# Weight rows stored as even and odd columns 2 KB apart, and read alternately by the products

## The chip, the cores and the metric

One core of one Trainium2 chip. The metric is the device time of one execution in microseconds (us); the kernel before was run three times. One further execution was taken by the hardware profiler: "the profile" and "the trace" mean that one.

## The reference

Two layers on a sequence of 256 frames with 2048 features; all inputs are float32. Each layer normalises, projects to 4096-wide parts, attends over 32 heads of 128, gates, projects back and adds to the residual. Cut to what matters:

```python
# first layer
h = rms_norm(x, a_norm)
q, k, v, g = jnp.split(h @ a_w_in, 4, axis=-1)             # 2048 -> 4 x 4096
o = chunked_relbias_attention(q, k, v, a_rel_bias)
x = x + (o * jax.nn.silu(g)) @ a_w_out                      # 4096 -> 2048
# second layer
h_kv = rms_norm(x, kv_norm)
k_s, v_s = jnp.split(h_kv @ kv_w, 2, axis=-1)               # 2048 -> 2 x 4096
cum_logf_h = cumsum(log_sigmoid(h_kv @ f_w + f_b))
q, g = jnp.split(rms_norm(x, b_norm) @ b_w_in, 2, axis=-1)  # 2048 -> 2 x 4096
o = forgetting_attention(q, k_s, v_s, cum_logf_h)
x = x + (o * jax.nn.silu(g)) @ b_w_out                      # 4096 -> 2048
return rms_norm(x, final_norm)
```

The projections are nearly all of the arithmetic. A product of float32 exactness is made of three products: each operand is split into a high part (rounded to the type fp32r) and a low part (the rest), and high x high, high x low and low x high are added up.

## The kernel before, in words

**The products.** The transposed activations are held on chip as high and low parts for the whole kernel (`Stat`: `xT`, `oA`, `x1T`, `oB`) and are the stationary operands, 128 x 128. The weights stream past them as the moving operand, 512 columns at a time (`UN`). `mm3` (lines 169 to 179) issues, for one row block of K (128 deep), the three products for each of the two halves of the sequence (`NT`): six matmuls at line 177. A `Unit` is 512 output columns with two accumulators; its `step` (346) takes one block of two rows of K (`KB`), and calls `mm3` for each.

**The weights' way.** The host cuts each weight matrix into units and blocks (`_units`, 958), so that one block is [128 partitions, 2 rows of K, 512 columns], 4 KB per partition in one run. `Feed` holds a list `todo` of all blocks in the order of use, written out at lines 306 to 334. `load` (190) issues a block's DMA from SyncE's queue into one of three `raw` tiles. `prepare` (211) splits it: ScalarE copies to the high part and VectorE subtracts (237, 238); in the second layer both also scale by the norm's gain, per row of K (233, 234). Four pairs of split tiles let TensorE run behind. A few blocks of the last projection are kept (`keep`).

**Quads.** In 15 of the 16 head groups of each layer the last block of both units is worked by a seven-product scheme (Strassen's, in a variant) in place of eight: `load_quad` (252) brings the two blocks side by side into `quad_raw`, `differ` (258) and `quad` (269) form differences and split them, and `products` (603) issues the 21 matmuls through `dot3` (426).

**Order.** The order of the work is fixed by the program: `drive` (682) and `project` (369) step the units, and between the steps advance the attention of the head group before (`attention`, 431), whose products are 256 or 128 columns wide. Nothing else sets it but the semaphores between the engines.

Of the kernel before, what the change touches and what calls it, by code (L numbers as in the profile page):

```python
# [9 lines left out]
F32 = mybir.dt.float32  # L10
F32R = mybir.dt.float32r
BF16 = mybir.dt.bfloat16
AF = mybir.ActivationFunctionType
OP = mybir.AluOpType
AX = mybir.AxisListType

P = 128
S = 256
NT = S // P
# [15 lines left out]
GC = HG * DH  # L35
UN = 512
KB = 2
SQ = 32
NQ = P // SQ
RAW = 3  # L40
SPLIT = 4
# [21 lines left out]

def r32(ap):
    return ap.bitcast(F32)


@with_exitstack
def trunk(ctx, tc, x, x_t, gains, a_w_in, a_rel, a_w_out, kv_w, f_w, f_b, b_w_in, b_w_out, final_norm, out):
# [5 lines left out]
    stream = ctx.enter_context(tc.tile_pool(name="stream", bufs=3))  # L75
# [9 lines left out]
    def big_tile(shape, dt, name):  # L85
        return big.tile(shape, dt, name=name, tag="big")
# [94 lines left out]
    class Feed:  # L181
# [8 lines left out]
        def load(self, spec, b, first):  # L190
            if self.early:
                raw = self.early.pop(0)
            else:
                raw = stream.tile([P, KB, UN], F32, name=f"{spec['name']}_raw{b}", tag="raw", bufs=RAW)
            for j in range(KB) if first else [slice(None)]:
                if first:
                    first(j)
                sp.dma_start(out=raw[:, j], in_=spec["w"][b][:, j])
            return raw

        def begin(self, first=None):
# [9 lines left out]
        def prepare(self, ahead=True, parts=(slice(None),)):  # L211
            if not self.loaded:
                self.begin()
            if not self.loaded:
                return
            spec, b, raw, (before, behind) = self.loaded.pop(0)
            if spec == "quad":
                self.quad(*b)
                self.refill()
                return  # L220
            if before:
                before()
            nm, h = spec["name"], b - (spec["nk"] // KB - spec["late"])
            if 0 <= h < spec["kept"]:
                both = big_tile([P, 2, KB, UN], F32R, f"{nm}_keep{b}")
                hi, lo = both[:, 0], both[:, 1]
            else:
                hi = stream.tile([P, KB, UN], F32R, name=f"{nm}_hi{b}", tag="hi", bufs=SPLIT)
                lo = stream.tile([P, KB, UN], F32R, name=f"{nm}_lo{b}", tag="lo", bufs=SPLIT)
            if spec["g0"] is not None:  # L230
                for j in range(KB):
                    gk = gain[:, spec["g0"] + b * KB + j:][:, :1]
                    act.activation(hi[:, j], raw[:, j], AF.Copy, scale=gk)  # L233
                    dve.scalar_tensor_tensor(lo[:, j], raw[:, j], gk, r32(hi[:, j]), op0=OP.mult, op1=OP.subtract)  # L234
                parts = ()
            for j in parts:
                act.activation(hi[:, j], raw[:, j], AF.Copy)  # L237
                dve.tensor_sub(lo[:, j], raw[:, j], r32(hi[:, j]))  # L238
            if behind:
                behind()  # L240
            self.ready.append((hi, lo))
            if ahead:
                self.refill()
# [8 lines left out]
        def load_quad(self, layer, g):  # L252
            q = quads[layer]
            for r in range(2):
                self.behind(q.raw[:, r, :, :1], -1)
                sp.dma_start(out=q.raw[:, r], in_=q.w(r, g))

        def differ(self, layer):

            q = quads[layer]  # L260
            raw, t = q.raw, q.t
            for r in range(2):
                for j in range(KB) if q.g0 else ():
                    act.activation(raw[:, r, j], raw[:, r, j], AF.Copy,
                                   scale=gain[:, q.g0[r] + QUAD * KB + j:][:, :1])
            dve.tensor_sub(t[:, 0], raw[:, 1], raw[:, :, 0])
            dve.tensor_sub(raw[:, 1, 0], raw[:, 1, 1], t[:, 0, 0])

        def quad(self, layer, i):


            raw, t = quads[layer].raw, quads[layer].t
            src = [raw[:, 0], t[:, 0], raw[:, 1, 1:], raw.rearrange("p a b n -> p (a b) n")[:, 1:3]][i]
            n = src.shape[1]
            hi = stream.tile([P, KB, UN], F32R, name=f"quad_hi{i}", tag="hi", bufs=SPLIT)
            lo = stream.tile([P, KB, UN], F32R, name=f"quad_lo{i}", tag="lo", bufs=SPLIT)
            act.activation(hi[:, :n], src, AF.Copy)
            dve.tensor_sub(lo[:, :n], src, r32(hi[:, :n]))
            if not i:
                dve.tensor_sub(raw[:, 0, 1], raw[:, 0, 1], raw[:, 1, 0])  # L280
            self.ready.append((hi, lo))

        def behind(self, dst, n):

            act.activation(dst, r32(self.ready[n][0][:, :, :1]), AF.Copy)

        def fill(self):
            while len(self.ready) <= DEPTH:
# [48 lines left out]
    class Unit:  # L337
# [8 lines left out]
        def step(self, b):  # L346
            hi, lo = feed.get()
            hold = b >= self.nk // KB - self.late
            if hold:
                self.held.append((b, hi, lo))  # L350
            for j in range(KB):
                mm3(self.acc, self.lhs, b * KB + j, range(1 if hold else NT), hi[:, j], lo[:, j], self.nk,
                    self.begun)
            self.left -= 1
            if not self.left:
                for b, hi, lo in self.held:
                    for j in range(KB):
                        mm3(self.acc, self.lhs, b * KB + j, [1], hi[:, j], lo[:, j], self.nk, self.begun)

    def unit(lhs):  # L360
        yield from rest(Unit(lhs, next(order)))
# [155 lines left out]
        return gs  # L517


    quad_raw, quad_t = (big_tile([P, 2, KB, UN], F32, name=f"quad{i}") for i in range(2))  # L520
    for both in (quad_raw, quad_t):
        feed.early += [both[:, 0], both[:, 1]]
    comb = big_tile([P, 2 * NT, UN], F32, name="comb")
    sums = big_tile([P, 2, 2, 4, P], F32R, name="sums")
    sq = [comb.rearrange("p a (k s) -> p (a k) s", s=S),
          quad_t.rearrange("p a b (k s) -> p (a b k) s", s=S)]
    xT = Stat("xT", KD)
    xr, homes = {}, iter(["wideh", "tb", "widel", "oT", "gs", "R", "Y", "Z", "wideh"])

# [48 lines left out]
    class Quads:  # L578
# [3 lines left out]
        def __init__(self, lhs, raw, t, comb, sums, w, g0=None):  # L582
            self.lhs, self.raw, self.t, self.comb, self.sums, self.w, self.g0 = lhs, raw, t, comb, sums, w, g0
            self.home = [v.rearrange("p (i c u) -> p i c u", i=NQ, u=SQ) for v in
                         (t[:, 1].rearrange("p b n -> p (b n)"), sums[:, 1].rearrange("p a k s -> p (a k s)"))]

        def sums_of_x(self):

# [14 lines left out]
        def products(self, first, second, scaled):  # L603


            comb = self.comb

            def x(k, t):
                return [v(QUAD * KB + k)[:, t * P:(t + 1) * P] for v in (self.lhs.h, self.lhs.l)]

            def sx(i):
                return self.sums[:, 0, 0, i], self.sums[:, 0, 1, i]

            def prod(acc, a, w, j, stop):
                dot3(acc, a, [v[:, j] for v in w], stop, stop)

            p1, p5, p7, p6 = (bank(n) for n in ("p1", "p5", "p7", "p6"))
            w = feed.get()
            prod(p1, x(0, 0), w, 0, True)
            prod(first.acc[0], x(1, 0), w, 1, False)  # L620
            w = feed.get()
            prod(p5, sx(0), w, 0, True)
            prod(p7, sx(2), w, 1, True)
            w = feed.get()
            dot3(second.acc[0], sx(3), [v[:, 0] for v in w], True, False)
            second.begun.add(0)
            w = feed.get()
            prod(first.acc[1], x(1, 1), w, 0, False)
            prod(p6, sx(1), w, 1, True)
            act.activation(comb[:, 0], p1, AF.Copy)  # L630
            dve.tensor_add(comb[:, 3], comb[:, 0], p6)
            dve.tensor_add(comb[:, 2], comb[:, 3], p5)
            dve.tensor_add(comb[:, 1], comb[:, 3], p7)
            dve.tensor_add(comb[:, 3], comb[:, 1], p5)
            rs, places = scaled
            for i, c1 in places:
                act.activation(comb[:, i, :c1], comb[:, i, :c1], AF.Copy, scale=rs[:, i % NT:i % NT + 1])
# [199 lines left out]
        yield  # L837


    b_tiles = [big_tile([P, 2, KB, UN], F32, name=f"b_quad{i}") for i in range(2)]  # L840
    b_tiles += [big_tile([P, 2 * NT, UN], F32, name="b_comb"), big_tile([P, 2, 2, 4, P], F32R, name="b_sums")]
    qb = quads["b"] = Quads(x1T, *b_tiles, lambda r, g: (b_w_in, kv_w)[r][g][QUAD], (GB, GKV))
    oB = Stat("oB", KI)
# [114 lines left out]
def _units(w, starts):  # L958

    k = w.shape[0] // P  # L960
    out = []
    for parts in starts:
        n = UN // len(parts)
        cols = np.concatenate([w[:, c:c + n] for c in parts], axis=1)
        out.append(cols.reshape(k // KB, KB, P, UN).transpose(0, 2, 1, 3))
    return np.ascontiguousarray(np.stack(out))


# [28 lines left out]
```

## Time and profile before

| | before |
|---|---|
| time, median of 3 runs | 1832.77 us (1830.29 to 1833.8) |
| span of the profiled execution | 1826.7 us |
| profiled execution's own time beside its span | not given by the page |
| mean granted TensorE clock | 0.998 |
| bytes moved, mean rate | 396.38 MB, 217 GB/s |

The engines are named as on the page: PE is TensorE's matmuls, PEld its weight loads, DVE is VectorE, ACT ScalarE, POOL GpSimd, SP SyncE. In a row of the groups stand the line, the engine, the operation, output and inputs, the shapes, the number of instructions, then the busy time in us, the mean length of one in ns, and the idle time of the engine just before them. A matmul's length there is from its start to its end, and successive matmuls overlap, so the distance between starts, not the length, is what one costs in a stream.

### The profile page before, as it was taken

To read this page: it belongs to the slowest core of one execution; us is meant where nothing else is said; L and a number is where in the kernel's file an instruction comes from. 1 tells how busy PE (TensorE), PEld (TensorE's weight loads), DVE (VectorE), ACT (ScalarE), POOL (GpSimd) and SP (SyncE) were. 2 spreads that over 40 slices of the span, in tenths; PEclk is the share of its full clock that TensorE was granted. 3 is DMA by queue.
4 is the path that set the end of the run, shared out by engine and by line. 5 is a ranking of instruction groups with operands and counts; after the bars stand their busy time and mean duration, and the time that the engine had idled before them with its cause. 6 is when DMAs were issued, how large, how long until landed. Compare 5 with 4: busy or idle time off the path is not lost.

```text
span 1826.7 us, 26015 instructions
## 1 busy us (share of the span) xinstructions
PE 1813.0 (99%) x8297; PEld 1507.2 (83%) x8297; DVE 1423.8 (78%) x2094; ACT 1196.3 (65%) x2245; POOL 521.8 (29%) x1071
## 2 busy tenths in 40 slices
PE   9999999999999999999999999999999999999998
PEld 7888888888888888888888888888888888888886
DVE  7887888888888787655568889888898989886544
ACT  6666666666666566545558777778777877775443
POOL 1333333333333333111104333333333333333000
PEclk9999999999999999999999999999999999999999
DMA  8666676666666766677766666666666666666664
GB/s 287 224 224 211 214 223 216 222 215 215 218 210 219 223 206 198 210 231 227 235 202 217 220 215 220 205 224 220 209 225 218 221 211 224 216 218 221 200 210 155
DMA packets 143145, 396.38 MB, mean 217 GB/s; under 512 B 31104, under 2 KB 37536, under 8 KB 142880
## 3 DMA queue, kind: packets, MB, share of 16 engines
q1 hardware_dynamic: 106960, 354.25, 59.0%
q0 software_dynamic: 32256, 37.29, 6.6%
q10 hardware_dynamic: 3792, 3.17, 0.6%
q8 instruction: 66, 1.08, 0.3%
q14 instruction: 71, 0.58, 0.1%
HBM read 351.05 MB, written 4.23 MB: 194 GB/s over the span
## 4 chain that ended last, share of the span: by engine, by line
PE 61%; DVE 1%; DMA 1%; ACT 1%; issue 1%; ACTq 0%; SPq 0%; DVEq 0%
PE bqg_acc L177 16%; PE bkv_acc L177 15%; PE bo_acc L177 10%; PE ao_acc L177 10%; PE avg_acc L177 2%; PE aqk_acc L177 2%; PE p L428 1%; PE p L429 1%; PE p L427 1%; DMA bqg_raw<-in_b_w_in 1%; PE op L485 1%; DVE bqg_lo L234 0%; PE s0p L451 0%; PE bqg_acc L429 0%; PE bqg_acc L428 0%
## 5 line engine op out<-in xcount | busy, mean ns | idle before, releaser
L400 POOL DMA_DIRECT2D sgZ<-sgY x512 | 250.5, 497 | 494.7 <-PE bkv_acc L177 188.1
L237 ACT ACTIVATE avg_hi<-avg_raw 128x1024 fp32r<-128x1024 f32 x112 | 118.5, 1058 | 125.8 <-DMA avg_raw<-in_a_w_in 82.8
L234 DVE SCALAR_TENSOR_TENSOR bkv_lo<-bkv_raw,gain,bkv_hi 128x512 fp32r<-128x512 f32 x226 | 159.2, 743 | 37.5 <-ACT bkv_hi L233 37.2
L238 DVE TENSOR_TENSOR avg_lo<-avg_raw,avg_hi 128x1024 fp32r<-128x1024 f32 x112 | 136.7, 1221 | 50.4 <-ACT avg_hi L237 49.9
L177 PE MATMUL bqg_acc<-bqg_hi,x1Th 128*128 128x512 f32 x452 | 174.1, 396 | 0.0
L177 PE MATMUL aqk_acc<-aqk_hi,xTh 128*128 128x512 f32 x452 | 172.4, 393 | 1.0 <-ACT aqk_hi L237 1.0
L233 ACT ACTIVATE bqg_hi<-bqg_raw,gain 128x512 fp32r<-128x512 f32 x226 | 150.3, 713 | 34.8 <-DMA bqg_raw<-in_b_w_in 18.0
L234 DVE SCALAR_TENSOR_TENSOR bqg_lo<-bqg_raw,gain,bqg_hi 128x512 fp32r<-128x512 f32 x226 | 162.7, 766 | 12.7 <-ACT bqg_hi L233 12.2
L177 PE MATMUL avg_acc<-avg_hi,xTh 128*128 128x512 f32 x452 | 172.3, 393 | 0.0
L177 PE MATMUL bqg_acc<-bqg_hi,x1Tl 128*128 128x512 f32 x452 | 171.4, 390 | 0.0
L177 PE MATMUL aqk_acc<-aqk_lo,xTh 128*128 128x512 f32 x452 | 170.9, 390 | 0.4 <-DVE aqk_lo L238 0.4
L177 PE MATMUL aqk_acc<-aqk_hi,xTl 128*128 128x512 f32 x452 | 171.0, 390 | 0.0
L177 PE MATMUL avg_acc<-avg_hi,xTl 128*128 128x512 f32 x452 | 170.9, 390 | 0.0
L177 PE MATMUL bkv_acc<-bkv_hi,x1Th 128*128 128x512 f32 x452 | 170.9, 390 | 0.0
L177 PE MATMUL bkv_acc<-bkv_hi,x1Tl 128*128 128x512 f32 x452 | 170.7, 389 | 0.0
L177 PE MATMUL bkv_acc<-bkv_lo,x1Th 128*128 128x512 f32 x452 | 170.6, 389 | 0.0
L177 PE MATMUL avg_acc<-avg_lo,xTh 128*128 128x512 f32 x452 | 170.6, 389 | 0.0
L177 PE MATMUL bqg_acc<-bqg_lo,x1Th 128*128 128x512 f32 x452 | 170.6, 389 | 0.0
L238 DVE TENSOR_TENSOR aqk_lo<-aqk_raw,aqk_hi 128x1024 fp32r<-128x1024 f32 x110 | 133.2, 1223 | 46.0 <-ACT aqk_hi L237 45.5
L233 ACT ACTIVATE bkv_hi<-bkv_raw,gain 128x512 fp32r<-128x512 f32 x226 | 150.1, 712 | 21.0 <-DMA bkv_raw<-in_kv_w 13.9
L400 POOL DMA_DIRECT2D b_sums<-b_quad x256 | 125.4, 498 | 132.3 <-PE bqg_acc L177 52.9
L400 POOL DMA_DIRECT2D sums<-quad x192 | 94.2, 498 | 206.4 <-PE avg_acc L177 79.8
(318 smaller groups left out, 4378.1 us busy)
## 6 DMA issues: line engine op xcount, KB each, us to landing
bqg_raw<-in_b_w_in SPq DMA_DIRECT2D x113, 512.0 KB, 4.0
bkv_raw<-in_kv_w SPq DMA_DIRECT2D x113, 512.0 KB, 4.7
avg_raw<-in_a_w_in SPq DMA_DIRECT2D x112, 512.0 KB, 5.2
aqk_raw<-in_a_w_in SPq DMA_DIRECT2D x110, 512.0 KB, 4.2
ao_raw<-in_a_w_out SPq DMA_DIRECT2D x64, 512.0 KB, 3.6
bo_raw<-in_b_w_out SPq DMA_DIRECT2D x64, 512.0 KB, 4.3
sgZ<-sgY POOLq DMA_DIRECT2D x512, 40.0 KB, 3.8
quad<-in_a_w_in SPq DMA_DIRECT2D x32, 512.0 KB, 5.9
```

What stands on the lines that cost most here:

```text
L177: pe.matmul(acc[t], x[:, t * P:(t + 1) * P], w, start=t not in begun, stop=k == nk - 1 and i == 2)
L233: act.activation(hi[:, j], raw[:, j], AF.Copy, scale=gk)
L234: dve.scalar_tensor_tensor(lo[:, j], raw[:, j], gk, r32(hi[:, j]), op0=OP.mult, op1=OP.subtract)
L237: act.activation(hi[:, j], raw[:, j], AF.Copy)
L238: dve.tensor_sub(lo[:, j], raw[:, j], r32(hi[:, j]))
L400: queues[j].dma_start(out=r32(z)[j * SQ:(j + 1) * SQ, i], in_=y[i * SQ:(i + 1) * SQ, j])
L427: pe.matmul(out_, a[0], b[0], start=start, stop=False)
L428: pe.matmul(out_, a[0], b[1], start=False, stop=False)
L429: pe.matmul(out_, a[1], b[0], start=False, stop=stop)
L485: pe.matmul(op[:, i, P:], v1[:, i * DH:(i + 1) * DH], pT[:, i, NT], start=False, stop=i == HG - 1)
```

## The change

Each row of 512 weights is stored as its 256 even columns and its 256 odd ones, and in a block of two rows of K the even halves of both rows stand first. A tile `[P, KB, UN]` becomes `[P, IL, KB, HN]` with `IL` = 2 and `HN` = 256: in a partition the run is even columns of row 0, even of row 1, odd of row 0, odd of row 1, 1 KB each. So columns 2n and 2n + 1 of a row lie 2 KB apart. The host stores the weights in that order (`_units`), so a block's transfer is the same 4 KB per partition. The new function `cols` hands a row to the matmul as the pattern (n, a): 256 times an even and an odd one in turn. The accumulators get their columns in the order of before, and nothing behind them changes. Splits of a whole block stay one run; where one row of K is split or scaled by itself, its two runs of 256 lie 2 KB apart. The quads' raw tile holds both blocks' even halves ahead of the odd ones (`[P, IL, 2, KB, HN]`), so that its rows too have their halves apart.

The core of the diff (the quads' differences and the first tiles are re-indexed in the same way and left out):

```diff
+IL = 2
+HN = UN // IL
...
+def cols(v, j):
+
+    return v[:, :, j].rearrange("p a n -> p n a")
...
-                raw = stream.tile([P, KB, UN], F32, name=f"{spec['name']}_raw{b}", tag="raw", bufs=RAW)
+                raw = stream.tile([P, IL, KB, HN], F32, name=f"{spec['name']}_raw{b}", tag="raw", bufs=RAW)
...
-                sp.dma_start(out=raw[:, j], in_=spec["w"][b][:, j])
+                sp.dma_start(out=raw[:, :, j], in_=spec["w"][b][:, :, j])
...
-                both = big_tile([P, 2, KB, UN], F32R, f"{nm}_keep{b}")
+                both = big_tile([P, 2, IL, KB, HN], F32R, f"{nm}_keep{b}")
...
-                hi = stream.tile([P, KB, UN], F32R, name=f"{nm}_hi{b}", tag="hi", bufs=SPLIT)
-                lo = stream.tile([P, KB, UN], F32R, name=f"{nm}_lo{b}", tag="lo", bufs=SPLIT)
+                hi = stream.tile([P, IL, KB, HN], F32R, name=f"{nm}_hi{b}", tag="hi", bufs=SPLIT)
+                lo = stream.tile([P, IL, KB, HN], F32R, name=f"{nm}_lo{b}", tag="lo", bufs=SPLIT)
...
-                    act.activation(hi[:, j], raw[:, j], AF.Copy, scale=gk)
-                    dve.scalar_tensor_tensor(lo[:, j], raw[:, j], gk, r32(hi[:, j]), op0=OP.mult, op1=OP.subtract)
+                    act.activation(hi[:, :, j], raw[:, :, j], AF.Copy, scale=gk)
+                    dve.scalar_tensor_tensor(lo[:, :, j], raw[:, :, j], gk, r32(hi[:, :, j]),
+                                             op0=OP.mult, op1=OP.subtract)
...
-                act.activation(hi[:, j], raw[:, j], AF.Copy)
-                dve.tensor_sub(lo[:, j], raw[:, j], r32(hi[:, j]))
+                act.activation(hi[:, :, j], raw[:, :, j], AF.Copy)
+                dve.tensor_sub(lo[:, :, j], raw[:, :, j], r32(hi[:, :, j]))
...
-                self.behind(q.raw[:, r, :, :1], -1)
-                sp.dma_start(out=q.raw[:, r], in_=q.w(r, g))
+                self.behind(q.raw[:, :, r, 0, :1], -1)
+                sp.dma_start(out=q.raw[:, :, r], in_=q.w(r, g))
...
-                mm3(self.acc, self.lhs, b * KB + j, range(1 if hold else NT), hi[:, j], lo[:, j], self.nk,
+                mm3(self.acc, self.lhs, b * KB + j, range(1 if hold else NT), cols(hi, j), cols(lo, j), self.nk,
                     self.begun)
...
-                        mm3(self.acc, self.lhs, b * KB + j, [1], hi[:, j], lo[:, j], self.nk, self.begun)
+                        mm3(self.acc, self.lhs, b * KB + j, [1], cols(hi, j), cols(lo, j), self.nk, self.begun)
...
-                dot3(acc, a, [v[:, j] for v in w], stop, stop)
+                dot3(acc, a, [cols(v, j) for v in w], stop, stop)
...
-        out.append(cols.reshape(k // KB, KB, P, UN).transpose(0, 2, 1, 3))
+        out.append(cols.reshape(k // KB, KB, P, HN, IL).transpose(0, 2, 4, 1, 3))
```

More of the change, by code (lines that the diff above doesn't have):

```diff
@@ L263, in differ @@
                 for j in range(KB) if q.g0 else ():
-                    act.activation(raw[:, r, j], raw[:, r, j], AF.Copy,
+                    act.activation(raw[:, :, r, j], raw[:, :, r, j], AF.Copy,
                                    scale=gain[:, q.g0[r] + QUAD * KB + j:][:, :1])
-            dve.tensor_sub(t[:, 0], raw[:, 1], raw[:, :, 0])
-            dve.tensor_sub(raw[:, 1, 0], raw[:, 1, 1], t[:, 0, 0])
+            dve.tensor_sub(t[:, 0], raw[:, :, 1], raw[:, :, :, 0])
+            dve.tensor_sub(raw[:, :, 1, 0], raw[:, :, 1, 1], t[:, 0, :, 0])
         def quad(self, layer, i):
             raw, t = quads[layer].raw, quads[layer].t
[L273 to L278, printed above, removed]
+            src = [raw[:, :, 0], t[:, 0], raw[:, :, 1, 1:], raw.rearrange("p a r j n -> p a (r j) n")[:, :, 1:3]][i]
+            n = src.shape[2]
+            hi = stream.tile([P, IL, KB, HN], F32R, name=f"quad_hi{i}", tag="hi", bufs=SPLIT)
+            lo = stream.tile([P, IL, KB, HN], F32R, name=f"quad_lo{i}", tag="lo", bufs=SPLIT)
+            act.activation(hi[:, :, :n], src, AF.Copy)
+            dve.tensor_sub(lo[:, :, :n], src, r32(hi[:, :, :n]))
             if not i:
-                dve.tensor_sub(raw[:, 0, 1], raw[:, 0, 1], raw[:, 1, 0])
+                dve.tensor_sub(raw[:, :, 0, 1], raw[:, :, 0, 1], raw[:, :, 1, 0])
             self.ready.append((hi, lo))
         def behind(self, dst, n):
-            act.activation(dst, r32(self.ready[n][0][:, :, :1]), AF.Copy)
+            act.activation(dst, r32(self.ready[n][0][:, :, 0, :1]), AF.Copy)
         def fill(self):
@@ L517, in gate_from @@
         return gs
-    quad_raw, quad_t = (big_tile([P, 2, KB, UN], F32, name=f"quad{i}") for i in range(2))
-    for both in (quad_raw, quad_t):
-        feed.early += [both[:, 0], both[:, 1]]
+    quad_raw = big_tile([P, IL, 2, KB, HN], F32, name="quad0")
+    quad_t = big_tile([P, 2, IL, KB, HN], F32, name="quad1")
+    feed.early += [quad_raw[:, :, 0], quad_raw[:, :, 1], quad_t[:, 0], quad_t[:, 1]]
     comb = big_tile([P, 2 * NT, UN], F32, name="comb")
@@ L525, in trunk @@
     sq = [comb.rearrange("p a (k s) -> p (a k) s", s=S),
-          quad_t.rearrange("p a b (k s) -> p (a b k) s", s=S)]
+          quad_t.rearrange("p r a j n -> p (r a j) n")]
     xT = Stat("xT", KD)
@@ L584, in __init__ @@
             self.home = [v.rearrange("p (i c u) -> p i c u", i=NQ, u=SQ) for v in
-                         (t[:, 1].rearrange("p b n -> p (b n)"), sums[:, 1].rearrange("p a k s -> p (a k s)"))]
+                         (t[:, 1].rearrange("p a j n -> p (a j n)"), sums[:, 1].rearrange("p a k s -> p (a k s)"))]
         def sums_of_x(self):
@@ L624, in products @@
             w = feed.get()
-            dot3(second.acc[0], sx(3), [v[:, 0] for v in w], True, False)
+            dot3(second.acc[0], sx(3), [cols(v, 0) for v in w], True, False)
             second.begun.add(0)
@@ L837, in forget @@
         yield
-    b_tiles = [big_tile([P, 2, KB, UN], F32, name=f"b_quad{i}") for i in range(2)]
+    b_tiles = [big_tile([P, IL, 2, KB, HN], F32, name="b_quad0"), big_tile([P, 2, IL, KB, HN], F32, name="b_quad1")]
     b_tiles += [big_tile([P, 2 * NT, UN], F32, name="b_comb"), big_tile([P, 2, 2, 4, P], F32R, name="b_sums")]
```

## The prediction

> **What bounds the kernel now.** I read the page's head first, then the table by stage, then the chain of work that ended last, and then the groups of TensorE by line. The head gives each engine's share of the span:
>
> ```profile
> span 1826.7 us, 26015 instructions
> PE 1813.0 (99%) x8297; PEld 1507.2 (83%) x8297; DVE 1423.8 (78%) x2094; ACT 1196.3 (65%) x2245; POOL 521.8 (29%) x1071
> ...
> PEclk9999999999999999999999999999999999999999
> DMA  8666676666666766677766666666666666666664
> ```
>
> TensorE is busy 99% of the span at the full granted clock, and no other engine comes near. A busy TensorE may still hide gaps inside its pipeline, so a stage and the distance from one product to the next decide. By stage, the columns after the length are PE, PEld, DVE, ACT and POOL with their instruction counts, then the clock and the DMA share:
>
> ```profile
> 1200.00:1400.00 200.00, 200.00 (x923) 166.84 (x922) 176.23 (x296) 160.86 (x342) 68.22 (x136) 1.00 0.66 222
> 1400.00:1600.00 200.00, 200.00 (x920) 166.73 (x919) 178.31 (x299) 157.65 (x325) 78.72 (x159) 1.00 0.67 220
> ```
>
> In the densest stretch (the second layer's groups) TensorE never rests and VectorE has 200 - 178.3 = 21.7 us spare. The chain shows the stream itself; each row is a start, a length and a count of back-to-back products:
>
> ```profile
> 759.18 149.65 PE ao_acc L177 x660
> ...
> 1303.16 19.04 PE bkv_acc L177 x84
> ...
> 1348.79 19.04 PE bkv_acc L177 x84
> ```
>
> 149.65 us / 660 = 226.7 ns and 19.04 us / 84 = 226.7 ns: one product of 512 columns starts every 226.7 ns in an output projection and in a group of the second layer alike. The two last rows are one head group apart: 45.6 us. The groups by line say whether anything interrupts that stream (the last figure is idle time ahead of the product), and how long the weight load beside it is:
>
> ```profile
> L177 PE MATMUL bqg_acc<-bqg_hi,x1Th 128*128 128x512 f32 x452 | 174.1, 396 | 0.0
> ...
> L177 PE MATMUL aqk_acc<-aqk_lo,xTh 128*128 128x512 f32 x452 | 170.9, 390 | 0.4 <-DVE aqk_lo L238 0.4
> ...
> L177 PE MATMUL ao_acc<-ao_hi,oAl 128*128 128x512 f32 x256 | 98.3, 389 | 0.0
> ```
>
> ```profile
> L177 PEld LDWEIGHTS bqg_acc<-bqg_lo,x1Th 128*128 128x128 f32 x452 | 85.0, 188 | 16.9
> ```
>
> No idle time, and the load (188 ns) fits inside the 226.7 ns. So the number of products times their distance is the time. The source gives the number: per layer 2 units x 16 plus 30 units x 14 rows of K = 452 rows, each 6 products (three of high and low parts for two halves of the sequence), 2712; 15 quads x 21 = 315; per output projection 4 x 32 x 6 = 768. Two of each: 2 x (2712 + 315 + 768) = 7590. The trace's x452 agrees. 7590 x 226.7 ns = 1720.7 us, 94% of the span; the rest is narrow attention products, the start and the end.
>
> The page gives a span and no time of its own. The runs' median, 1832.8 us, lies 6.1 us above the span, and I add every term to that median.
>
> **The change part by part.**
>
> *The instructions.* Nothing is added, removed or moved on any queue: the list for each engine has the same rows in the same order, and shapes alone differ (128x512 becomes 128x2x256 where one row of K is handled, a quad's load 128x1024 becomes 128x2x512). So no wait appears, and no instruction passes another.
>
> *The moving operand, all 7590 products.* The 512 columns that stream through the array were one run of 2 KB; now each next 4-byte element lies 2 KB away from the last. The trace of before has no operand on any engine read in that way, so the price is bounded by rows. First, what a column costs. Products of 256 columns stand beside those of 512:
>
> ```profile
> 1008.29 0.28 PE L427 MATMUL op<-wideh,vh 128*128 128x256 f32 x1
> ...
> 1008.88 0.28 PE L429 MATMUL op<-wideh,vl 128*128 128x256 f32 x1
> 1009.00 0.61 PE L485 MATMUL op<-sgZ,v 128*128 128x128 f32 x4
> ```
>
> ```profile
> L428 PE MATMUL op<-widel,vh 128*128 128x256 f32 x64 | 18.6, 291 | 1.1 <-DVE widel L420 1.1
> ...
> L427 PE MATMUL op<-wideh,vh 128*128 128x256 f32 x64 | 17.9, 280 | 0.0
> ```
>
> Six of 256 columns take 1009.00 - 1008.29 = 0.71 us, 118 ns each, so 256 further columns cost 226.7 - 118.3 = 108.4 ns, 0.423 ns a column. By the mean durations (389 against about 285 ns, the middle of 280 and 291) it is 104 ns, 0.406. I take 0.416: 213 ns of the 226.7 are columns and about 13.7 are fixed.
>
> The lower end is no cost. Below nothing is excluded, since nothing on the path gets shorter. For the upper end I take the dearest price at which an engine here reads the memory on chip column by column, VectorE's subtraction of two such operands:
>
> ```profile
> L238 DVE TENSOR_TENSOR avg_lo<-avg_raw,avg_hi 128x1024 fp32r<-128x1024 f32 x112 | 136.7, 1221 | 50.4 <-ACT avg_hi L237 49.9
> ...
> L238 DVE TENSOR_TENSOR avg_lo<-quad,avg_hi 128x512 fp32r<-128x512 f32 x2 | 1.3, 688 | 0.1
> ```
>
> Its slope is (1221 - 688) / 512 = 1.04 ns a column, and with its fixed part 1221 / 1024 = 1.19. At 1.19 a product takes 512 x 1.19 + 13.7 = 623 ns, which is 396 more, and 7590 x 0.396 = 3006 us.
>
> Between zero and 3006 us I take one step of the stream per element in place of one per two: TensorE's 0.416 ns a column is under half of VectorE's 1.04, which fits a port that fetches two neighbours at once and can't when they are 2 KB apart. That doubles the columns' part: 226.7 + 213 = 440 ns a product, 7590 x 0.213 = 1617 us, and 1832.8 + 1617 = **3450 us**. If the fixed 13.7 ns hide under the longer stream it is 104 us less; with 0.423 a column it is 28 more. So this case by itself spans 3340 to 3490.
>
> The Trainium skill speaks against the change here: "SBUF — State Buffer", section "Specifications (TRN2)", says that the memory works in lines of 16 bytes, that a line must be hit at least twice for full bandwidth, and that each crossing to a new line is penalised. Here every element crosses. The page gives no size for a penalty, and no row of before shows one.
>
> *Splitting on ScalarE and VectorE.* One row of K is now two runs of 256, in the second layer's scaled splits, in the quads and in the first four loads; whole blocks stay one run of 1024. I cost it at nothing, under the product stream. If a break cost as much as a second instruction, the bound is two of 256 columns against one of 512:
>
> ```profile
> L420 DVE TENSOR_TENSOR widel<-sgZ,wideh 128x256 fp32r<-128x256 f32 x64 | 25.1, 415 | 0.6 <-ACT wideh L419 0.6
> ...
> L234 DVE SCALAR_TENSOR_TENSOR bqg_lo<-bqg_raw,gain,bqg_hi 128x512 fp32r<-128x512 f32 x226 | 162.7, 766 | 12.7 <-ACT bqg_hi L233 12.2
> ```
>
> 2 x 415 - 688 = 142 ns for some 31 such instructions of a group (28 in its two units, three in its quad), 4.4 us. VectorE's spare time per group is 21.7 x 45.6 / 200 = 4.9 us, so even then it just fits at today's product distance, and far more easily at 440 ns.
>
> *Loads.* A block is still 4 KB a partition in one run. Only a quad's load (now two runs of 2 KB) and the first four (1 KB runs) break up:
>
> ```profile
> quad<-in_a_w_in SPq DMA_DIRECT2D x32, 512.0 KB, 5.9
> ```
>
> There are 32 + 30 quad loads, on a DMA share of 0.66, issued four steps or more before they are read: nothing.
>
> *Start and end.* The last wait is short and holds no weights: the chain ends so:
>
> ```profile
> 1779.80 38.09 PE bo_acc L177 x168
> ...
> 1820.38 1.33 ACT xg L933 x2
> ```
>
> Products run until 1817.9; some 9 us of closing work stay as they are.
>
> **The rivals.**
>
> *The hop is free.* The place is the moving operand's read; the price is nothing, and it decides as long as a lone element can be fetched in 0.416 ns or fetches from the two streams are held and used twice. For it: a whole product has one pattern fixed ahead, and the two streams each run on without a break. Against it: no row shows any engine reading faster than that. The time is 1832.8 us plus the split terms, which fit under the stream: 1830 to 1834. The same time comes out if the change doesn't do what it says, say if the two dimensions of the pattern were read one after the other; the instruction list shows one product for each as before, and the output's columns would come out permuted, so I give that little of the weight.
>
> For this rival there is a measurement in the Trainium skill: "Vector Engine (DVE) Microarchitecture Reference", section "5.2 Measured stream behaviour on trn2 (trn3 not measured)", reports that a single VectorE stream that alternated between two regions every element kept its full rate, though a two-source operation with a hop at every element slowed from 1.054 to 1.73 ns a column. No run here shows either yet.
>
> *A lone element costs as much as a run of four.* The mechanism: the stream is fed by wide fetches that a contiguous run uses up entirely, four elements each, and an alternating one for a single element. Then the columns' part is taken four times: 4 x 213 + 13.7 = 866 ns, 639 more, 7590 x 0.639 = 4850 us, and 6683 us in all. It decides if such a fetch can't be had more often than every 4 x 0.416 = 1.66 ns. Against it: VectorE gets an element from each of two streams every 1.04 ns, if contiguous ones. The 16-byte line that "SBUF — State Buffer" names is four such elements, so this is the harsher reading of its rule.
>
> *A fixed time per hop, between the two.* If a lone element comes at VectorE's rate, 1.04 to 1.19 ns, a product takes 546 to 623 ns, and the whole 1832.8 + 7590 x (0.319 to 0.396) = 4254 to 4839 us.
>
> *A part of the hops is hidden* by a small buffer: anything between 1834 and 3340.
>
> **How the numbers follow.** Doubled columns 0.46; free 0.21; four times 0.15; a fixed time between double and VectorE's dearest rate 0.12; partly hidden 0.05; 0.01 for a gain that I can't name. The predicted time is that of the likeliest, 3450 us. A range that leaves out only the fourfold case and the gain holds 0.84: from 1829, the free case with the spread of the runs, to 4840, the upper bound. It is wide because it takes in cases on both sides; the likeliest alone has 3340 to 3490. A measurement of this kernel can tell about 0.2% (3.7 us) from no change: the free case lies mostly within that (0.19), with 0.01 above and 0.01 below it; so slower 0.46 + 0.15 + 0.12 + 0.05 + 0.01 = 0.79, the same 0.19, faster 0.02.
>
> **What would show it.** In the chain of the changed kernel a run of products divided by its count gives the distance: 440 ns for my case, 226.7 for free, 546 to 623 for the fixed time, 866 for four times. Products of 256 columns must keep their 118 ns, since their operands are unchanged. Busy time of VectorE and ScalarE should stay near 1424 and 1196 us while their shares halve; if a two-run split costs, the rows of the scaled subtraction show it (766 ns now). I am wrong if the distance is 227, if the span grows with the distance unchanged (then a wait has appeared, and the idle column names it), or if the growth is not the same for every row of 512 columns.

## The result, and the profile after

| | before | changed |
|---|---|---|
| median of 20 runs each | 1829.78 us (1825.81 to 1836.81) | 1819.99 us (1806.75 to 1835.46) |
| ratio | | 0.9943 (95% interval 0.9927 to 0.9959) |
| span of the profiled execution | 1826.7 us | 1824.8 us |

The forecast was 3450 us. The kernel became 0.6% faster. Ratios, here and below, leave out executions in a slow state: one of the 20 changed ones (1835.46 us), one of `op_later`'s four (2609.34 us) and one of the kernel before beside `halves` to `step2` (3724.22 us). The profiled execution of the changed kernel lies high among its runs and shows only 1.9 us of the gain; it still shows what happened. From its page:

```profile
span 1824.8 us, 26015 instructions
PE 1771.9 (97%) x8297; PEld 1534.1 (84%) x8297; DVE 1420.1 (78%) x2094; ACT 1184.8 (65%) x2245; POOL 522.0 (29%) x1071
...
PE 29%; DMA 13%; DVE 12%; ACT 7%; issue 4%; POOL 0%; ACTq 0%; SPq 0%; DVEq 0%
```

The last line gives the shares of the chain that ended last. Before, it read:

```profile
PE 61%; DVE 1%; DMA 1%; ACT 1%; issue 1%; ACTq 0%; SPq 0%; DVEq 0%
```

TensorE now rests for 52.9 us of the span, against 13.7 before, and the chain, nearly all TensorE's before, runs through loads, VectorE and ScalarE too. The stream itself, in the chain of the changed kernel (start, length, count), in the same output projection as before:

```profile
756.85 142.45 PE ao_acc L184 x660
```

142.45 us / 660 = 215.8 ns a product; before it was 226.7. So the hop costs nothing, and the product is 10.9 ns shorter: over 7590 products 83 us, of which about 10 arrived. Where the rest went shows in a wait ahead of the value products of the attention (`op`), on VectorE's split of the probabilities (`widel`), and behind it. First the rows of the tables of waits, before and after, in us in total, number, longest; then one place in order of time; then the same place in a table by stretch, where the granted clock is the number behind the busy time and its count:

```profile
PE op L428 <- DVE widel L420: 1.1, 3, 0.5
...
PE op L436 <- DVE widel L428: 25.9, 31, 2.6
```

```profile
1227.42 0.47 PE L436 MATMUL op<-widel,vh 128*128 128x256 f32 x1 [2.46 <-DVE widel L428]
...
1230.23 0.63 PE L184 MATMUL bqg_acc<-bqg_lo,x1Th 128*128 128x512 f32 x1
1230.66 0.55 PE L184 MATMUL bqg_acc<-bqg_hi,x1Tl 128*128 128x512 f32 x1
...
1231.48 0.38 PE L184 MATMUL bqg_acc<-bqg_hi,x1Tl 128*128 128x512 f32 x1
1231.69 0.38 PE L184 MATMUL bqg_acc<-bqg_hi,x1Th 128*128 128x512 f32 x1
```

```profile
1224.00:1227.00 3.00, 0.96 (x5) 1.00 0.55 175
1227.00:1228.00 1.00, 0.57 (x3) 0.79 0.12 33
1228.00:1231.00 3.00, 2.96 (x11) 0.50 0.24 68
1231.00:1234.00 3.00, 3.00 (x15) 1.00 0.24 69
```

TensorE waits 2.46 us, and then has half the clock granted for 3.41 us: two products start 430 ns apart there (1230.23 and 1230.66), and 210 ns once the clock is back. The trace has eleven such stretches ahead of the last product, each behind an idle time of 1.1 to 2.6 us; half of 3.41 us, about 1.7 us, is lost in each on top of the wait, by estimate. Not every wait of that length is followed by one: two, of 1.33 and 1.46 us, are not (the start left aside). The stretches start whole multiples of 3.413 us apart, as if on a fixed grid. In this trace each cell of that grid in which TensorE idled 1.25 us or more in all is followed by a stretch, and none in which it idled 1.16 us or less; the traces of the runs below keep the grid, but not so sharp a line (in kb1 a cell with 2.00 us idle has none behind it). So where a wait falls on the grid matters beside its length. Before, these products waited 1.1 us in all and the clock did not drop ahead of the last product. Taking every distance between the starts of two products that is over 60 ns above the median for its width, from 60 us to the last product, the excess is 12.1 us before and 90.1 us after: 78 us of new waits, slow stretches included, against 83 us of shorter products.

### The profile page after: what moved, and what is told of

The parts are those of the page before. It is cut to its first block, busy times and chain, and to the rows that moved or that the text cites. A ratio compares the mean times of both kernels' runs of the same rounds, so it can differ in the third digit from the quotient of the medians.

```text
span 1824.8 us, 26015 instructions
## 1 busy us (share of the span) xinstructions
PE 1771.9 (97%) x8297; PEld 1534.1 (84%) x8297; DVE 1420.1 (78%) x2094; ACT 1184.8 (65%) x2245; POOL 522.0 (29%) x1071
## 4 chain that ended last, share of the span: by engine, by line
PE 29%; DMA 13%; DVE 12%; ACT 7%; issue 4%; POOL 0%; ACTq 0%; SPq 0%; DVEq 0%
PE ao_acc L184 8%; PE bo_acc L184 7%; PE bqg_acc L184 6%; DMA bkv_raw<-in_kv_w 4%; DVE bqg_lo L241 3%; DMA bqg_raw<-in_b_w_in 3%; DVE bkv_lo L241 2%; PE bkv_acc L184 2%; ACT bkv_hi L240 2%; DMA cb<-cumd 2%; ACT bqg_hi L240 1%; DVE quad_lo L286 1%; DVE qk L650 1%; DMA bo_raw<-in_b_w_out 1%; PE op L493 1%
## 5 line engine op out<-in xcount | busy, mean ns | idle before, releaser
L184 PE MATMUL aqk_acc<-aqk_hi,xTh 128*128 128x512 f32 x452 | 168.3, 384 | 1.0 <-ACT aqk_hi L245 1.0
L184 PE MATMUL avg_acc<-avg_hi,xTh 128*128 128x512 f32 x452 | 168.0, 383 | 0.0
L184 PE MATMUL aqk_acc<-aqk_lo,xTh 128*128 128x512 f32 x452 | 166.8, 381 | 1.2 <-DVE aqk_lo L246 1.2
L184 PE MATMUL aqk_acc<-aqk_hi,xTl 128*128 128x512 f32 x452 | 166.8, 381 | 0.0
L184 PE MATMUL avg_acc<-avg_lo,xTh 128*128 128x512 f32 x452 | 166.6, 380 | 0.0
L184 PE MATMUL avg_acc<-avg_hi,xTl 128*128 128x512 f32 x452 | 166.5, 380 | 0.0
L184 PE MATMUL bkv_acc<-bkv_hi,x1Th 128*128 128x512 f32 x452 | 166.3, 379 | 0.0
L184 PE MATMUL bkv_acc<-bkv_hi,x1Tl 128*128 128x512 f32 x452 | 166.1, 379 | 0.0
L184 PE MATMUL bkv_acc<-bkv_lo,x1Th 128*128 128x512 f32 x452 | 166.1, 379 | 0.0
```

The lines of the kernel that those rows point to most:

```text
L184: pe.matmul(acc[t], x[:, t * P:(t + 1) * P], w, start=t not in begun, stop=k == nk - 1 and i == 2)
```

## The experiments

Two things had to be explained: why lone elements 2 KB apart are read faster than a contiguous row, and where the gain went. "Distance" is the start-to-start distance of products of 512 columns in the profile, from a run of products in the chain where one is shown. Products of 256 columns, read contiguously in all kernels, kept 118 to 120 ns in every run below except where they waited.

### What is it in the way of reading?

Four kernels change only the order in which a row's 512 elements are stored and read; the products and their results stay.

**halves**: the row as two runs of 256, 2 KB apart.

```diff
-    return v[:, :, j].rearrange("p a n -> p n a")
+    return v[:, :, j]
```

> Each row of 512 read as two runs of 256, the first 256 columns and then the last 256, 2 KB apart; the storage is otherwise that of the changed kernel. Theory A (the shape of the pattern: a moving operand that is a single run costs some 11 ns more per product, whatever the run holds): distance 216 ns and a time like the changed kernel's, about 1820 us. Theory B (the neighbours: each fetch of adjacent elements costs, lone elements don't): distance 227 ns, time like before, 1830 us. Theory C (the two streams: alternating between two places spreads the fetches): distance 227 ns, since the places change once per product.

Distance 226.7 ns (149.65 us / 660 in the chain); 1833.3 us, ratio 1.0025 (1.0014 to 1.0036). Two dimensions in the pattern are not what helps: theory A falls.

**runs2** and **runs4**: two (four) neighbours from one half, then two (four) from the other.

```diff
-    return v[:, :, j].rearrange("p a n -> p n a")
+    return v[:, :, j].rearrange("p a (n m) -> p n a m", m=2)
```

> Each row read in pairs: two neighbouring elements from one half, two from the other, the halves 2 KB apart. Theory A (shape): 216 ns. Theory B (neighbours): 227 ns. Theory C (two streams): 216 ns, as the places alternate at every pair.

> Each row read in runs of four elements (16 bytes) from the two halves in turn, 2 KB apart. Theory A (shape): 216 ns. Theory B (neighbours): 227 ns. Theory C (two streams): 216 ns. If pairs and fours differ, the width of a fetch lies between them.

Pairs: 2595.0 us, ratio 1.419 (1.417 to 1.421). Fours: 1996.4 us, ratio 1.092 (1.090 to 1.093), distance 250 ns. The chain with pairs:

```profile
1076.18 216.70 PE ao_acc L184 x660
```

216.70 / 660 = 328.3 ns. None of the three theories had this: a pattern with more neighbours in it is dearer than the one with none.

**step2**: the row stays in one stretch; all even elements are read first, then all odd ones.

```diff
+def cols(v):
+    return v.rearrange("p (n a) -> p a n", a=2)
```

> Made from the kernel before: each row stays one stretch of 2 KB, and is read as all its even elements, then all its odd ones, so that the elements that follow each other are 8 bytes apart and no two are neighbours. Theory A (shape): 216 ns. Theory B (neighbours): 216 ns. Theory C (two streams): 227 ns, since there is one stream at a time. If lone elements 8 bytes apart cost a fetch each, it is far above 227 ns.

3521.3 us, ratio 1.925 (1.922 to 1.929), and in the chain:

```profile
1457.81 297.74 PE ao_acc L182 x660
```

297.74 / 660 = 451.1 ns: the doubling that was forecast for the change, brought about by a step of 8 bytes. A, B and C had 216 or 227; all three fall as written down, and what costs is neither the hop nor the lone element as such. Only the last sentence of the expectation, a fetch for each lone element 8 bytes apart, had it.

**kb1**, **swap**, **four**: the two streams 1 KB apart inside the row (tiles, loads and splits as before the change); each pair of neighbours read backwards; four streams in place of two.

```diff
+    return v.rearrange("p (a n) -> p n a", a=2)              # kb1
+    return v.rearrange("p (n a) -> p n a", a=2)[:, :, ::-1]  # swap
-IL = 2
+IL = 4                                                       # four, in the changed kernel
```

> Even and odd columns stored 1 KB apart inside the row's own 2 KB and read alternately; tiles, loads and splits are those of before. Theory D (the pattern: an innermost dimension of two elements is fetched two at a time, wherever they lie): distance 216 ns. Theory E (what was fetched is held: an element's neighbour is served from a held fetch if at most one other place was read in between): 216 ns. Theory F (the distance of 2 KB is what spreads the two streams): another distance between products, 227 to 451 ns. By D and E the time is that of the changed kernel, about 1820 us, and the two-run splits and loads had no part in it.

> Each pair of neighbours stored swapped and read backwards, second element first: innermost dimension of two elements, every pair contiguous in one stretch of 2 KB. Theory D (pairs as a pattern): 216 ns. Theory E (held fetches): 216 to 227 ns, since both elements come from one fetch. If alternating between two places is what helps (F), 227 ns or more.

> As the changed kernel with four streams in place of two: columns 4n to 4n + 3 lie 1 KB apart each, and the innermost dimension has four elements. Theory D (two at a time, wherever they lie): 216 ns. Theory E (one other place held): 451 ns like lone elements; if four fetches are held, 216 ns. Time by 216 ns about 1820 us, by 451 ns about 3520 us.

kb1: 215.8 ns; 1817.3 us, ratio 0.9921 (0.9893 to 0.9949). swap: 226.7 ns; 1829.4 us, ratio 0.9987 (0.9972 to 1.0003). four: 283.3 ns; 2246.2 us, ratio 1.226 (1.225 to 1.228). D falls by swap and by four, F by kb1. E, in the form written down, had 216 or 451 for four streams and saw neither. kb1 also shows that the shorter product owes nothing to the splits in two runs and the loads of the change: without them the distance is the same, and so, within the intervals, is the time.

**patterns**: the way of reading by itself. Ahead of the kernel before stand trains of 40 products of zeros, one for each pattern.

```diff
+        o, s, m = go([[2, 256], [1024, 2]], 0)
+        for i in range(40):
+            pe.matmul(o, s, m, start=i == 0, stop=i == 39)
```

> The kernel before with 27 trains of 40 products of zeros put ahead of it, one train for each way of reading the moving operand; read from the distances of their starts, not from the time. Theory R (the operand is read by two readers in turn, one for the 1st, 3rd, 5th element and one for the 2nd, 4th, 6th; each needs two elements in a row from one line of 16 bytes for full speed): alternating at 8, 16, 32 bytes, 1 KB and 2 KB: 216 to 227 ns; two streams that each step by 8 bytes: 216 to 227 (two hits a line for each reader); two streams that each step by 16 bytes: 451; one stream in steps of 8 bytes and one in steps of 16 bytes: both 451; backwards: 227. Theory W (words of 8 bytes are fetched once and two are held): alternating anywhere 216; two streams in 8-byte steps 451, since each element has a word to itself; in 16-byte steps 451; one stream in 8 or 16-byte steps 451. So two streams in 8-byte steps tell them apart. The fixed part: one run of 512, 256 and 128 against alternating ones: if the 11 ns are a start cost, they are the same at each length; if a rate, they shrink with it. In bf16, two elements are 4 bytes: by R all but the step of 16 bytes are 216.

A train's busy time runs from the first start to the last end, so (busy - mean length) / 39 is its distance. In this order: two streams stepping by 16 bytes each, one stream stepping by 8 bytes, the two streams stepping by 8 bytes, alternating at 16 bytes, one run of 256 columns, and 256 alternating:

```profile
L142 PE MATMUL bench_ps<-bench 128*128 128x512 f32 x40 | 18.3, 632 | 0.0
...
L145 PE MATMUL bench_ps<-bench 128*128 128x512 f32 x40 | 18.3, 632 | 0.0
...
L139 PE MATMUL bench_ps<-bench 128*128 128x512 f32 x40 | 9.2, 389 | 0.0
...
L133 PE MATMUL bench_ps<-bench 128*128 128x512 f32 x40 | 8.8, 379 | 0.0
...
L178 PE MATMUL bench_ps<-bench 128*128 128x256 f32 x40 | 5.0, 283 | 0.0
L181 PE MATMUL bench_ps<-bench 128*128 128x256 f32 x40 | 4.6, 275 | 0.0
```

(18.3 - 0.632) / 39 = 453 ns for the first two, 226 for two streams in steps of 8 bytes, 216 for alternating. All fp32r trains, by the trace's starts (the first, one run, began with seven products some 430 ns or more apart; the value is that of the others):

| fp32r, 512 columns | distance, ns |
|---|---|
| one run; from the second, from the third element; backwards | 227; 237; 233; 233 |
| alternating 2 KB, 1 KB, 32 B, 16 B apart | 216 each |
| alternating 8 B apart; pairs swapped | 227; 227 |
| two streams in steps of 8 B; of 16 B | 227; 453 |
| one stream in steps of 8 B; of 16 B | 453; 461 |
| runs of 2, 4, 8 from two places | 340, 250, 243 |
| four streams 1 KB apart; 16 B apart | 283; 268 |
| 256 columns: one run; alternating | 120; 112 |
| 128 columns: one run; alternating | 112; 112 |

Two streams in steps of 8 bytes were to tell R from W: 227 ns, where R had 216 to 227 and W 451. W falls. R, two readers in turn, fits the rows without jumps back to within 10 ns: with one run each reader gets two elements of every 16-byte line, with a step of 8 bytes in one stream only one, with two streams alternating all four. If a reader needs about 1.77 ns for each new line (an estimate, 227 ns / 128 lines), one run takes 128 x 1.77 = 227 ns by construction, and a step of 8 bytes 256 x 1.77 = 453, as measured; alternating needs half the lines per reader and falls to the 216 ns that something else sets. By R the 11 ns of a contiguous row are a line rate, just too slow, and not a start cost. The shorter trains don't decide that: at 256 columns the difference is 8 ns, between the 5.5 of a rate and the 11 of a start cost, and the alternating train there stands at 112 ns, as both do at 128, so a floor may hide a part. The Trainium skill's page "SBUF — State Buffer", section "Specifications (TRN2)", speaks of lines of 16 bytes that want at least two hits for full bandwidth. Applied to each of two readers, that agrees with the doubling at one hit a line (453 ns); two hits gave 227 ns, though, and four 216. R stays a model. Taken as written it would have 453 for pairs and for four streams, where 340 and 268 to 283 were measured, and 227 for runs of 4 and 8, which took 250 and 243; and in bf16 it failed. There the trains were 216 ns for one run, 226 in steps of 4 bytes and 900 in steps of 16, but 484 for alternating at 1 KB, where R had 216.

### Where did the gain go?

**op_later**: the changed kernel with the value products one block of weights later in TensorE's order.

```diff
-            finish(old) if i >= last else advance(old)
+            finish(old) if i >= 2 else advance(old, not i)
```

> The changed kernel with the last products of the attention (the value products) one block of weights later in the order of TensorE, in both layers. Theory G (the gain went into the wait ahead of these products, 27 us, and the halved clock behind it, some 16 us in the second layer): the time falls to 1775 to 1790 us. Theory H (the head groups are bound by another engine or by the loads, and the wait only shows there): the wait moves to other products and the time stays within 1810 to 1825 us.

1804.4 us, ratio 0.9848 (0.9826 to 0.9870): between the ranges of G and H. The wait ahead of the value products fell from 25.9 to 1.2 us, and the excess of all distances from 90.1 to 67.9 us; waits ahead of the score products (`s1p`) took a part of the place:

```profile
PE s1p L435 <- ACT q1h L427: 11.7, 13, 2.6
PE s1p L437 <- DVE q1l L428: 7.2, 3, 3.4
...
PE op L436 <- DVE widel L428: 1.2, 1, 1.2
```

**before_op**: the same edit in the kernel before.

> The kernel before with the value products one block later, without the change of the weights' layout. Theory G (the wait exists only because the products' stream got faster): 1826 to 1833 us, no change, since these products waited 1.1 us there. If the later place is a gain by itself, the time falls by more than 10 us as it did with the change.

1827.1 us, ratio 0.9984 (0.9972 to 0.9996): nearly nothing, as G had it. The later place pays with the shorter products alone.

**best1** and **best2**: kb1 with that edit, and the split of queries and keys one block earlier in the first layer; best2 also has the score products of the second layer one block later.

```diff
-QK7_STEPS = {0: 1, 5: 1, 6: 2}
+QK7_STEPS = {0: 1, 4: 1, 6: 2}
-B1_STEPS = {2: 1, 3: 1, 5: 2}
+B1_STEPS = {2: 1, 3: 1, 6: 2}     # best2 alone
```

> Columns alternating 1 KB apart, value products one block later, and in the first layer the split of queries and keys one block earlier. Theory G (the waits lie on the attention's products, each a matter of its place): 1785 to 1797 us, since the waits ahead of the score products there, some 20 us, shrink. Theory H (another engine bounds the group): 1800 to 1806 us, as with the value products alone.

> As best1, and in the second layer the score products one block later. Theory G: a few us less than best1, as some 14 us of waits ahead of the score products there shrink. Theory H: as best1.

best1: 1798.1 us, ratio 0.9828 (0.9811 to 0.9845). best2: 1821.7 us, ratio 0.9954 (0.9936 to 0.9971). best1 lies between the ranges, 1 us above G's and 2 below H's; best2, which by G was to gain a few us more and by H nothing, lost 24. With the score products later in the second layer, the value products wait again (11.7 us on `widel`), and the excess is 90.3 us, against 67.1 in best1 and 67.9 in `op_later`. Each further edit moved the waits; their sum stayed, or rose. That speaks for a shared cause.

**kb1_op**, **half_lo**, **before_half_lo**: kb1 with the value products later and nothing else; the same with the low part formed for one row of K in two (the second row's products use the first row's low part, so a part of the sum is left out); the kernel before with the same left out.

```diff
-                    dve.scalar_tensor_tensor(lo[:, j], raw[:, j], gk, ...)
+                    if not j:
+                        dve.scalar_tensor_tensor(lo[:, j], raw[:, j], gk, ...)
...
-                dve.tensor_sub(lo[:, j], raw[:, j], r32(hi[:, j]))
+                if j != 1:
+                    z = 0 if j == 0 else slice(0, 1)
+                    dve.tensor_sub(lo[:, z], raw[:, z], r32(hi[:, z]))
```

> Columns alternating 1 KB apart inside each row and the value products one block later, nothing else: the simplest form of the changed kernel with the later place. Both theories: like op_later, 1800 to 1805 us; if the splits in two runs cost anything there, 2 to 4 us less.

> kb1_op, but VectorE forms the low part of only the first of the two rows of K in each block, and the products use it for both rows: the low parts of every second row are left out. TensorE has the same products in the same order. Theory G (what is left of the waits is a matter of the places in TensorE's order): 1795 to 1805 us, as kb1_op. Theory H (the waits are for VectorE's queue, in which the attention's steps stand behind the splits): the waits fall from some 70 us to under 25, and the time to 1750 to 1765 us, close to the 1748 us that the shorter products allow.

> The kernel before with the same low parts left out. By both theories there is nothing to gain, since TensorE's stream bounds it: 1825 to 1833 us.

kb1_op: 1790.9 us, ratio 0.9791 (0.9761 to 0.9822), the fastest whole kernel of the study, 9 us below what both theories had. half_lo: 1743.3 us, ratio 0.9529 (0.9510 to 0.9548), 7 us below even H's range. before_half_lo: 1822.7 us, ratio 0.9964 (0.9951 to 0.9977), a small gain where nothing was expected. The table by stage (TensorE, its loads, VectorE, ScalarE, GpSimd, clock, DMA share) of kb1_op:

```profile
1200.00:1400.00 200.00, 196.41 (x931) 171.81 (x930) 178.31 (x298) 157.76 (x327) 78.95 (x162) 0.98 0.66 216
```

and of half_lo:

```profile
1200.00:1400.00 200.00, 200.00 (x970) 176.45 (x969) 143.25 (x242) 161.96 (x345) 79.22 (x163) 1.00 0.69 230
```

With VectorE's share of the stage down from 89% to 72%, TensorE never rests, the clock holds, and 970 matmuls fit where 931 did. Over the whole kernel the excess of the distances is 10.6 us (12.1 before the change). The same relief is worth 6 us in the kernel before, and 48 us here (1790.9 - 1743.3). The loads carry more in that stage, not less (share 0.69 against 0.66). So the gain was lost in waiting for VectorE, as H has it.

How VectorE holds TensorE up without being full shows at the place of above. VectorE in order of time, and, from the changed kernel's table of SyncE's waits, what its loads wait for most:

```profile
1221.91 1.42 DVE L241 SCALAR_TENSOR_TENSOR bqg_lo<-bqg_raw,gain,bqg_hi 128x512 fp32r<-128x512 f32 x2 [1.75 <-ACT bqg_hi L240]
...
1225.85 1.18 DVE L286 TENSOR_TENSOR quad_lo<-b_quad,quad_hi 128x1024 fp32r<-128x1024 f32 x1
1226.95 0.41 DVE L428 TENSOR_TENSOR widel<-sgZ,wideh 128x256 fp32r<-128x256 f32 x1
```

```profile
SPq L205 <- DVE bqg_lo L241: 293.4, 95, 13.7
```

The split that TensorE waits for (`widel`) comes behind a quad's split and 5 us of work without a break. Ahead of that work VectorE stood idle for 1.75 us, for ScalarE's half of a weight split, which had waited 2.82 us for a load; and that load went out at 1215.54 us, right behind a split on VectorE that SyncE had waited for (ended 1215.48). So there are two ways: the attention's steps stand in VectorE's queue behind splits, as H says, and a late split makes the next load late. half_lo shortens both; no run separates them, and none with more `raw` tiles was made.

## Why the prediction was wrong

*What bounds the kernel now* was right: 7590 products at 226.7 ns, other engines behind. Everything multiplied with that number was sound, and it made the error large. Only "no other engine comes near" was not: the table under it has VectorE at 178.31 of 200 us.

*The moving operand* is the step that failed: "which fits a port that fetches two neighbours at once and can't when they are 2 KB apart. That doubles the columns' part". The hop costs 0 ns and the product fell to 215.8. The price was inferred from one ratio, TensorE's 0.416 ns a column against VectorE's 1.04, with no row behind the mechanism. The doubling exists, at 451 ns (step2; my sum had 440), but for a step of 8 bytes in one stream. By model R it comes when elements that follow at a distance of two lie in different 16-byte lines, and here they are neighbours within their stream; why a product is priced so stays a model.

*"Below nothing is excluded, since nothing on the path gets shorter"* failed too. A product of 226.7 ns was no floor: 10.9 ns of it went. Whether they came from the 13.7 ns that I called fixed or from the columns' part, the trains leave open. 118 ns at 256 columns could not show it, since those are read contiguously too (120 ns in the trains, 112 alternating).

*The line rule* of the Trainium skill's page "SBUF — State Buffer", section "Specifications (TRN2)", two hits for each line, I read as one stream of elements: "every element crosses". If R is right, the count that matters is the hits of each half of the elements, and by that count the change improves it, from two to four.

*The free hop*, chance 0.21, was nearest in time, 1832.8 us, but that is in part luck: its distance, 226.7 ns, was wrong by 10.9 ns, and new waits took back most of the 83 us. Its argument that the two streams each run on without a break fits two streams of fp32r, but not four streams (283 ns) or bf16 (484). The measured 1820 us lies below the range's lower end of 1829 for want of a case with a gain that could be named; 0.02 stood on faster.

*Splits and loads at nothing* held for the change itself: kb1 has neither and takes the same time within the intervals. With the value products later it did not: kb1_op is 13.5 us faster than `op_later`, which differs from it in the weights' layout alone, and with it in the two-run splits and the quads' loads; no run says which of these it is. The splits' own length hardly shows it: the scaled subtraction (`bqg_lo`, 766 ns before) takes 767 ns in `op_later` and 766 in kb1_op. The cover, too, was narrower than it looked: 21.7 us of VectorE's 200 in the second layer were called spare and used to hide splits. That margin was not used up, since VectorE was busy 169.9 us of the same stage in the changed kernel; its idle time came where the next split was not ready, and behind it the attention was late. "So no wait appears" was reasoned from the list of instructions, and the step that asked what is late next was made only for a longer stream, not for a shorter one.

*What would show it* worked: a run of products in the chain divided by its count gave the answer at once.

## What to carry to other kernels

Price an operand's way of reading by a train of 40 products of that pattern before sizing it by a ratio; here five patterns that look alike range from 216 to 453 ns. Before a bound is loosened, ask which engine is nearly full beside it: waits on VectorE, 89% busy in the densest stage, swallowed most of 83 us, and moving the value products helped once, while further moves only shifted the waits. A TensorE wait of 1.1 to 2.6 us can be followed by half clock for 3.41 us, so short waits cost more than their length.

## What the runs showed of the hardware that was not expected

- A contiguous fp32r row of 512 is not the fastest moving operand: 227 ns a product, against 216 if two streams at least 16 bytes apart alternate element by element.
- A step of 8 bytes doubles the product (451 to 453 ns), and runs of two neighbours from two places cost 328 to 340, more than no neighbours at all.
- In bf16 it is the other way round: one run 216 ns, alternating at 1 KB 484, a step of 16 bytes 900. Why is open, as are the prices of runs of 2, 4 and 8 and of four streams.
- Waits of 1.1 to 2.6 us ahead of one product were followed by a stretch of 3.41 us at granted clock 0.50, eleven times in the changed kernel. The stretches start on a grid of 3.413 us, and two other waits, of 1.33 and 1.46 us, had none behind them.
